# The value projection's last 16 tokens in one stationary tile

## The chip, the cores and the metric

The kernel runs on one core of a Trainium2 chip. The metric is the device time of one execution in microseconds (us); the time before is the median of three runs. The engines are TensorE (PE in the profile, its weight loads PEld), VectorE (DVE), ScalarE (ACT), GpSimd (POOL) and SyncE (SP, which issues DMAs). Each engine works through its own queue of instructions in order; an instruction that waits for another engine holds up what stands behind it.

## What is computed

Two layers of a decoder. In each, a mixer (attention with a forget gate, a convolution module, a short gated convolution) is followed by a feed-forward part. With 16 meta tokens ahead of 512 there are L = 528 tokens of 1024 features.

```python
u = rms_norm(h, pre_g)
z = jnp.einsum("bld,de->ble", u, w_in)
q, k, v, f_logit, a_val, a_gate, sc_b, sc_c, sc_x = jnp.split(z, idx, axis=-1)
log_f = jax.nn.log_sigmoid((f_logit + b_forget).astype(jnp.float32))
y_attn = forgetting_attention(q.reshape(hs), k.reshape(hs), v.reshape(hs), log_f)
```

The change touches the product that makes v (512 columns, 8 heads of 64) and f_logit (8 columns).

## The kernel before

Each float32 operand of a product is kept as two tiles, a rounded one (hi) and the remainder (lo), and a product is made as three: hi x hi, hi x lo and lo x hi, all added up in one PSUM bank. The normalised input u is held as `uhi` and `ulo`, 128 features by 8 k tiles by 528 tokens.

`v_proj(j)` makes v for four heads at a time (j = 0 and 1; for j = 0 with the 8 columns of the forget gate, so 264 columns, else 256). Its stationary operand is u, its moving operand the weights, so the tokens come out on the partitions: 528 tokens are four blocks of 128 (b = 0 to 3) and one of 16 (b = 4). Each block is 8 k tiles x 3 = 24 products (line 1407) into one of the three banks that the ring "mm" hands round; q, k and the other projections use the same ring. When a block is done, `out` (line 1389) copies v on ACT into `vals` (line 1392), and for j = 0 adds the gate's bias on DVE into `fx` (line 1396); both read the block's bank, and the bank is free when both have ended. `forget_gate` starts when all five `fx` are there: some small operations on ACT and DVE, the last of DVE's being the additions into `fpre` (line 1435), and then the products of lines 1439 and 1440 on PE.

The tiles of the mixer are set up on POOL just before, by `mset` (a memset, line 448), in the order of the code: `vals`, `fx`, `p4`, `causal`, then the four `kh` and `qh` pairs, then `dm0` and `dm1`. In both layers the value projection with j = 0 is the first work on PE after them.

What sets the order on the other engines is a planner. A call of `act(...)`, `dve(...)` or `gp(...)` hands it an operation with an estimated duration, what it waits for and a priority (lower goes first); a generator such as `v_proj` yields after each k tile, and the planner's clock `flow` decides which thread's products, and which operation of which engine, are emitted next. An engine's queue then has that order on the chip, whatever the real times are. Calls made outside the planner, such as the memsets of `mset`, cost nothing on its clock. The planner has DVE fill the gaps between urgent operations with the convolution's taps (line 1153, 60 per layer, in two chains) and has ACT and DVE split the coming weights (lines 789 and 793).

`y_pair(i)` hands out a pair of tiles of 128 x 528 from eight tags; the mixer's outputs are kept in them. `y_pair(7)` is written only near the end of the mixer.

Of the kernel before, what the change touches and what calls it, by code (L numbers as in the profile page):

```python
# [10 lines left out]
F32 = mybir.dt.float32  # L11
# [5 lines left out]
P = 128  # L17
D = 1024
KD = D // P
L = 528  # L20
# [3 lines left out]
HEADS = 8  # L24
DH = 64
# [43 lines left out]
_COLS = {}  # L69
# [287 lines left out]
def mm_us(n, k=P):  # L357

    return max(n / 2400 + 0.012, 0.00086 * k)
# [7 lines left out]
def act_us(n):  # L367
    return 0.17 + 0.0009 * n


def dve_us(n):
    return 0.17 + 0.00101 * n


def stt_us(n):
    return 0.22 + 0.00102 * n
# [13 lines left out]
def tile_hybrid_trunk(ctx: ExitStack, tc: tile.TileContext, xT, wflat, pv_d, out):  # L390
    nc = tc.nc
# [3 lines left out]
    def T(pool, shape, dt, tag, bufs=None):  # L395
        uid[0] += 1
        kw = {} if bufs is None else {"bufs": bufs}
        return pool.tile(list(shape), dt, tag=tag, name=f"{tag}_{uid[0]}", **kw)
# [29 lines left out]
    def mmt(i=None):  # L428

        if i is None:  # L430
            i = PAIRS[n_pairs[0] % 2]
            n_pairs[0] += 1
        return psum[:, i:i + 2]
# [4 lines left out]
    for l in range(DEPTH):  # L438
        pv = T(const, [P, NPV], F32, f"pv{l}")
# [7 lines left out]
    def mset(t, val):  # L447
        nc.gpsimd.memset(t.bitcast(F32), val)
# [33 lines left out]
    flow = Flow()  # L482


    uhi = T(keep, [P, KD, L], F32R, "uhi")
    ulo = T(keep, [P, KD, L], F32R, "ulo")
# [4 lines left out]
    def load_h(pool, src, prio=0):  # L491

        t = T(pool, [P, KD, L], F32, "h", 1)
        at = {(hf, k0): flow.op("sp", dma_us(2 * H), lambda k0=k0, hf=hf: nc.sync.dma_start(
            t[:, k0:k0 + 2, half_sl(hf)], src[:, k0:k0 + 2, half_sl(hf)]), prio=prio + 3 * hf, lat=dma_lat(2 * H))
            for hf in range(2) for k0 in range(0, KD, 2)}
        return t, at
# [187 lines left out]
    def next_w():  # L685
        prefetch(1 + AHEAD)
        return ready.popleft()[1]

    def act(us, fn, *after, **kw):
        return flow.op("act", us, fn, after, **kw)  # L690

    def dve(us, fn, *after, **kw):
        return flow.op("dve", us, fn, after, **kw)

    def gp(us, fn, *after, **kw):
        return flow.op("pool", us, fn, after, **kw)
# [127 lines left out]
    def flow_w():  # L824

        b = blocks_w(1)[0]
        yield [b.tok]
        return b
# [17 lines left out]
    def two(t):  # L846
        return t.rearrange("p (a b) -> p a b", a=2)
# [277 lines left out]
    def mixer(l, ypool, first, close_first, spans, front, rzs, u_at):  # L1125
        pv, pg = pvs[l]
# [119 lines left out]
        ap = ms.enter_context(tc.tile_pool(name=f"ap{l}", bufs=1, side="right", reuse_waits="tile"))  # L1246
# [4 lines left out]
        def bank(kind):  # L1251

            slot = yield from flow.grab(banks[kind])
            return psum[:, slot.buf], slot
# [83 lines left out]
        vals = T(ap, [P, 5, HEADS, VW], F32, "vals")  # L1338
        mset(vals[:, 4], 0.0)
        mset(vals[:, :, :, DH:], 1.0)  # L1340
        fx = T(ap, [P, 5, HEADS], F32, "fx")
# [31 lines left out]
        for j in range(2):  # L1373
            dm = T(ap, [P, L], F32R, f"dm{j}")
            mset(dm[:, :N_META], 0.0)
            dms.append(dm)
        g_hl = [T(mp, [P, L], F32, "sq", 2)[:HEADS].bitcast(F32R) for _ in range(2)]

        v_at = {}

        def v_proj(j):
            blks = []
            for _ in range(2):
                blks.append((yield from flow_w()))
            wv = [b.w for b in blks]
            nw = wv[0][0].shape[-1]
            fs, vs = [], []

            def out(b, n, ps, tok):
                src = ps[:n, :256].rearrange("p (h d) -> p h d", d=DH)  # L1390
                c = _COLS["b_forget"]
                a = act(act_us(256), lambda: nc.scalar.copy(vals[:n, b, 4 * j:4 * j + 4, :DH], src), tok)
                r = []
                vs.append(a)
                if nw > 256:
                    r.append(dve(0.2, lambda: nc.vector.tensor_add(fx[:n, b, :], ps[:n, 256:nw], pv[:n, c:c + HEADS]),
                                 tok, prio=0))
                    fs.append(r[-1])
                return [a] + r

            for b in range(5):
                n = min(P, L - P * b)
                ps, slot = yield from bank("mm")
                for k in range(KD):
                    w = wv[k // 4]
                    for p, (wi, ui) in enumerate(((0, 0), (0, 1), (1, 0))):
                        nc.tensor.matmul(ps[:n, :nw],  # L1407
                                         lhsT=(uhi, ulo)[ui][:, k, P * b:P * b + n],
                                         rhs=w[wi][:, k % 4, :],
                                         start=k == 0 and p == 0, stop=k == KD - 1 and p == 2)  # L1410
                    tok = flow.mm(3 * mm_us(nw))
                    if k < KD - 1:
                        yield
                if b == 4:
                    for blk in blks:
                        blk.slot.close(tok)
                slot.close(*out(b, n, ps, tok))
                yield
            v_at[j] = vs
            if nw > 256:  # L1420
                flow.thread(forget_gate(fs), True)
# [391 lines left out]
        def fill():  # L1813

            for kind, j in mixer_steps(l)[2:]:
                if kind == "v":
                    yield from v_proj(j)
                elif kind == "q":
                    yield from q_proj(j)
                elif kind == "k":  # L1820
                    yield from k_proj(j)
                elif kind == "pw":
                    blk = yield from flow_w()
                    flow.thread(conv_tail(blk), True)
                else:
                    if j == 1 and kind == "sc_c":
                        yield [When(lambda: [zero] if 0 in sc_done else None)]
                    yield from proj({"sc_c": sc_c, "sc_x": sc_x, "sc_b": sc_b}[kind](j))
# [17 lines left out]
        for i, f in enumerate(sums_at(l, 1)):  # L1846
            copies, *adds = sum_steps(l, f)
            tok = flow.op("sp", 2.0, copies, (Tok(flow.pe + SUM_AT[i]),), prio=8, lat=SUM_LAT)
            for op in adds:
                tok = gp(SUM_US, op, tok, prio=8, lat=SUM_LAT)  # L1850
# [169 lines left out]
    def y_pair(i):  # L2020
        t = T(ypool, [P, 2, L], F32R, f"y{i}")
        return t[:, 0], t[:, 1]
# [6 lines left out]
    with tc.tile_pool(name="pre", bufs=2, reuse_waits="tile") as sp, tc.manual_schedule(engines=every):  # L2029
# [7 lines left out]
        h, h_at = load_h(sp, xT)  # L2037
# [5 lines left out]
        for k in range(KD):  # L2043
            hk, hi, lo, gc = h[:, k, :H], u_raw[0][k], u_raw[1][k], g0[:, k:k + 1]
            c = act(act_us(H) + 0.06, lambda hk=hk, hi=hi, gc=gc: nc.scalar.activation(hi, hk, AF.Copy, scale=gc),
                    h_at[0, k - k % 2], prio=0)
            d = dve(stt_us(H), lambda hk=hk, hi=hi, lo=lo, gc=gc: nc.vector.scalar_tensor_tensor(
                lo, in0=hk, scalar=gc, in1=hi.bitcast(F32), op0=ALU.mult, op1=ALU.subtract), c, prio=0)
# [45 lines left out]
    for l in range(DEPTH):  # L2094
        pv, pg = pvs[l]
# [14 lines left out]
        with ms, tc.manual_schedule(engines=every):  # L2110
            flow.yields = YM
            y, y_at, early = mixer(l, ypool, first, close_pools, i_spans, front, rzs, u_at)
# [5 lines left out]
        with tc.tile_pool(name=f"fp{l}", bufs=2, reuse_waits="tile") as fp:  # L2118
# [35 lines left out]
            with tc.manual_schedule(engines=every):  # L2154
                flow.yields = YF
                h, h_at = load_h(fp, xT if l == 0 else h_dram)
# [188 lines left out]
            for part, nf in enumerate(PARTS):  # L2345
                for f in range(f0, f0 + nf):
# [15 lines left out]
                    for i in (2 * f, 2 * f + 1):  # L2362
# [5 lines left out]
                        w = next_w()  # L2368
                        ps = mmt((6, 2)[i % 2]) if ts else mmt()
# [17 lines left out]
                if part < len(PARTS) - 1:  # L2387
# [3 lines left out]
                    for some in ((0, 1), *((m,) for m in range(2, KD))):  # L2391
# [12 lines left out]
                        for m, ps in zip(some, tiles):  # L2404
                            if final:
                                d, src = yp[:, m, t0:], ps[:, 0, :2 * fw]
                            else:
                                d, src = two(yp[:, m, t0:]), ps[:, :, :fw]
# [82 lines left out]
```

## Time and profile before

| | us |
|---|---|
| three runs | 1262.51, 1263.30, 1263.05 |
| median | 1263.05 |
| span of the profiled execution | 1262.4 |
| granted TensorE clock, mean | 0.999 |
| value projection j = 0, first layer, on PE | 49.10 to 63.5 |
| value projection j = 0, second layer, on PE | 676.96 to 691.5 |
| value projection j = 1, first layer, among attention | 123.3 to 149 |

The profile is that of one execution; it gives its span, from the first to the last instruction, and no other time of it. All times in rows are us from the start of the span. A timeline row has the start, the time busy, the engine and line, the operation, what it writes and reads (out<-in), sizes and count, and in brackets the idle time of the engine just before and what ended it. "x3" is three instructions in one row. A row of the waits has the engine and line that waited and what it waited for, the total, the count and the longest. A row of groups ends with the busy time and mean ns of one, and the idle time before. A PE product's time overlaps with its neighbours', so that the distance of two starts, and not the length, is what one costs.

### The profile page before, as it was taken

The page shows a single profiled execution, that of the slowest core. Times are in us where ns is not written, and L with a number is a line of the kernel's source. Part 1 is how long each engine was busy: PE and PEld are TensorE (multiplying, and loading weights), DVE is VectorE, ACT ScalarE, POOL GpSimd, SP SyncE. Part 2 cuts the span into 40 slices and gives each one's busy share as a digit, 9 for nine tenths or more (in the row PEclk, how much of TensorE's full clock was granted, in tenths as well). Part 3 has the DMA queues.
Part 4 walks back from the last instruction along what each step waited for, and adds up shares of the span by engine and source line. Part 5 has one row for each costly group of instructions (what it writes and reads, how often), then busy time and mean ns, then how long its engine had stood idle before and what let it go on. Part 6 is the DMA issues. An engine that isn't in the chain of part 4 may idle for free.

```text
span 1262.4 us, 24292 instructions
## 1 busy us (share of the span) xinstructions
PE 1243.7 (99%) x9554; PEld 1194.0 (95%) x9554; DVE 926.1 (73%) x1581; ACT 710.3 (56%) x1377; POOL 174.6 (14%) x360
## 2 busy tenths in 40 slices
PE   8999999999999999999999999999999999999997
PEld 8998898999999999999999988999999899989997
DVE  7887866589874776487688878656799748756964
ACT  7254576655444663476673545775554447526763
POOL 1323411001111001010003244120021000000000
PEclk9999999999999999999999999999999999999999
DMA  7357551726648755776652584547166565465611
GB/s 245 82 155 173 126 119 44 259 87 149 186 147 334 244 193 149 240 195 169 208 189 67 156 194 110 144 111 241 71 163 176 146 218 170 153 223 182 203 60 67
DMA packets 80755, 206.59 MB, mean 164 GB/s; under 512 B 8624, under 2 KB 18992, under 8 KB 80128
## 3 DMA queue, kind: packets, MB, share of 16 engines
q1 hardware_dynamic: 66976, 168.20, 42.1%
q0 software_dynamic: 13664, 36.84, 13.0%
q8 instruction: 75, 1.23, 0.4%
q14 instruction: 40, 0.33, 0.1%
HBM read 170.82 MB, written 50.60 MB: 175 GB/s over the span
## 4 chain that ended last, share of the span: by engine, by line
PE 89%; DVE 3%; issue 3%; DMA 2%; ACT 2%; POOL 1%; SPq 0%; DVEq 0%; POOLq 0%; ACTq 0%
PE psum L837 58%; PE psum L2288 17%; PE psum L1407 5%; PE psum L1671 3%; PE psum L1637 2%; PE psum L974 1%; PE psum L1593 1%; DMA raw<-in_w_dram 1%; PE psum L1737 1%; PE psum L1323 1%; DMA w_split<-slo 0%; DMA h<-in_w_dram 0%; POOL dm L1608 0%; DVE yp L1050 0%; DMA h<-in_x_dram 0%
## 5 line engine op out<-in xcount | busy, mean ns | idle before, releaser
L837 PE MATMUL psum<-y,whi 128*128 128x264 f32 (+3 forms) x1968 | 383.8, 299 | 0.8 <-DVE zs L989 0.7
L837 PEld LDWEIGHTS psum<-y,whi 128*128 128x128 f32 x1968 | 305.6, 188 | 13.8 <-DVE zs L989 0.9
L837 PE MATMUL psum<-uhi,whi 128*128 128x264 f32 (+1 forms) x1168 | 292.1, 289 | 1.5 <-ACT uhi L2069 0.7
L837 PE MATMUL psum<-ulo,whi 128*128 128x264 f32 (+1 forms) x1168 | 285.7, 284 | 0.6 <-DVE ulo L2071 0.4
L837 PE MATMUL psum<-uhi,wlo 128*128 128x264 f32 (+1 forms) x1168 | 285.1, 283 | 0.0
L837 PE MATMUL psum<-y,wlo 128*128 128x264 f32 (+3 forms) x984 | 273.7, 297 | 0.3 <-DVE wlo L793 0.3
L837 PEld LDWEIGHTS psum<-uhi,whi 128*128 128x128 f32 x1168 | 201.5, 188 | 6.2 <-issue 1.6
L837 PEld LDWEIGHTS psum<-ulo,whi 128*128 128x128 f32 x1168 | 201.6, 188 | 1.3 <-DVE ulo L2071 0.6
L837 PEld LDWEIGHTS psum<-uhi,wlo 128*128 128x128 f32 x1168 | 201.3, 188 | 0.0
L837 PEld LDWEIGHTS psum<-y,wlo 128*128 128x128 f32 x984 | 177.8, 188 | 5.8 <-DVE wlo L793 0.6
L2173 DVE SCALAR_TENSOR_TENSOR c<-zs,pv,c 128x528 f32<-128x528 f32 (+1 forms) x176 | 130.6, 756 | 23.5 <-ACT c L2171 22.2
L652 ACT CAST whi<-raw 128x1024 fp32r<-128x1024 f32 (+1 forms) x65 | 66.1, 1020 | 97.1 <-PE psum L837 74.5
L793 DVE TENSOR_TENSOR wlo<-raw,whi 128x1024 fp32r<-128x1024 f32 (+2 forms) x80 | 95.6, 1203 | 29.7 <-ACT whi L789 29.2
L789 ACT CAST whi<-raw 128x1024 fp32r<-128x1024 f32 (+2 forms) x80 | 81.7, 1031 | 24.9 <-PE psum L837 18.0
L653 DVE TENSOR_TENSOR wlo<-raw,whi 128x1024 fp32r<-128x1024 f32 (+1 forms) x65 | 76.9, 1183 | 21.1 <-ACT whi L652 21.0
L1153 DVE SCALAR_TENSOR_TENSOR cacc<-apad,pv,cacc 128x528 f32<-128x528 f32 x120 | 87.6, 772 | 0.1
L2288 PE MATMUL psum<-uhi,whi 128*128 128x258 f32 (+1 forms) x252 | 71.3, 284 | 0.0
L2288 PE MATMUL psum<-ulo,whi 128*128 128x258 f32 (+1 forms) x252 | 71.2, 283 | 0.0
L2288 PE MATMUL psum<-uhi,wlo 128*128 128x258 f32 (+1 forms) x252 | 70.7, 283 | 0.0
L2171 ACT ACTIVATE c<-zs,pv 128x528 f32<-128x528 f32 (+1 forms) x88 | 63.0, 727 | 6.8 <-DVE zs L2136 2.7
L2206 POOL COPY cols<-y 128x1 f32<-128x1 f32 x24 | 17.2, 716 | 335.8 <-ACT y L2187 335.5
L2288 PE MATMUL psum<-t,shi 128*128 128x258 f32 (+1 forms) x336 | 63.2, 283 | 0.0
(273 smaller groups left out, 2323.9 us busy)
## 6 DMA issues: line engine op xcount, KB each, us to landing
raw<-in_w_dram SPq DMA_DIRECT2D x114, 512.0 KB, 4.5
raw<-in_w_dram SPq DMA_DIRECT2D x30, 448.0 KB, 5.1
h<-in_w_dram SPq DMA_DIRECT2D x25, 512.0 KB, 4.5
raw<-w_sum SPq DMA_DIRECT2D x21, 512.0 KB, 5.4
h<-w_sum SPq DMA_DIRECT2D x21, 512.0 KB, 4.8
h<-in_w_dram POOLq DMA_DIRECT2D x16, 512.0 KB, 4.6
w_sum<-h POOLq DMA_DIRECT2D x16, 512.0 KB, 6.4
w_sum<-in_w_dram SPq DMA_DIRECT2D x26, 256.0 KB, 5.2
```

The costliest lines, as they stand in the source:

```text
L652: nc.scalar.copy(hi[:, :sz], raw[:, :sz])
L653: last_low[0] = nc.vector.tensor_sub(lo[:, :sz], raw[:, :sz], hi[:, :sz].bitcast(F32))
L789: nc.scalar.copy(box["hi"][:, :sz], box["raw"][:, :sz])
L793: nc.vector.tensor_sub(lo[:, :sz], box["raw"][:, :sz], box["hi"][:, :sz].bitcast(F32))
L837: nc.tensor.matmul(d, lhsT=w[a][:, k, cols], rhs=rhs(b, k, hf), start=start and i == 0 and p == 0, stop=stop and i == n - 1 and p == 2)
L1153: nc.vector.scalar_tensor_tensor(conv[j], in0=src, in1=conv[j], scalar=col("a_dw_w", CK * j + i), op0=ALU.mult, op1=ALU.add)
L1407: nc.tensor.matmul(ps[:n, :nw], lhsT=(uhi, ulo)[ui][:, k, P * b:P * b + n], rhs=w[wi][:, k % 4, :], start=k == 0 and p == 0, stop=k == KD ...
L1637: nc.tensor.matmul(s, lhsT=k[:, ka:ka + kn], rhs=q[:, s0:qz], start=i == 0, stop=i == 1)
L1671: nc.tensor.matmul(acc[:, s0 - qa:qz - qa], lhsT=vals[:, b].rearrange("p h d -> p (h d)")[:, o:o + P], rhs=box["p"], start=b == 0, stop=b ...
L2171: nc.scalar.activation(dst, src[:, 2:2 + 2 * fw], AF.Copy, scale=wtap(2, t))
L2173: nc.vector.scalar_tensor_tensor(dst, in0=src[:, i:i + 2 * fw], scalar=wtap(i, t), in1=dst, op0=ALU.mult, op1=ALU.add)
L2288: nc.tensor.matmul(psum[:, bank, :n7], lhsT=w[a][:, k0 + k, :], rhs=rhs(b, k), start=start and k == 0 and p == 0, stop=stop and k == K2 - ...
```

## The change

For the block of 16 tokens, the high and the low part of u are put side by side in one stationary tile: 48 columns, high in 0 to 15, zeros in 16 to 31, low in 32 to 47. One product with the high weights then makes both hi x hi and lo x hi, on partitions 0 to 15 and 32 to 47 of the bank; a second with the low weights makes hi x lo (and lo x lo beside it). So 16 products take the place of 24, and the rows from partition 32 on are added to the first ones at the end (`out_tail`): an ACT copy into `low`, then one DVE add for v and two small ones for the gate. The tile is borrowed from `y_pair(7)`: a memset on POOL and two ACT copies, asked for once in a layer, ahead of the value projection.

```diff
@@ -1374,6 +1374,11 @@
             dm = T(ap, [P, L], F32R, f"dm{j}")
             mset(dm[:, :N_META], 0.0)
             dms.append(dm)
+        spare_y = y_pair(KD - 1)[0]
+        tail_u = spare_y[:, :KD * 48].rearrange("p (k n) -> p k n", n=48)
+        mset(tail_u, 0.0)
+        tail_at = [act(0.3, lambda i=i, t=t: nc.scalar.copy(tail_u[:, :, 32 * i:32 * i + L - 4 * P], t[:, :, 4 * P:]), prio=2)
+                   for i, t in enumerate((uhi, ulo))]
         g_hl = [T(mp, [P, L], F32, "sq", 2)[:HEADS].bitcast(F32R) for _ in range(2)]
 
         v_at = {}
@@ -1386,7 +1391,25 @@
             nw = wv[0][0].shape[-1]
             fs, vs = [], []
 
+            def out_tail(b, n, ps, tok):
+                to = vals[:n, b, 4 * j:4 * j + 4, :DH]
+                src = ps[:n, :256].rearrange("p (h d) -> p h d", d=DH)
+                c = _COLS["b_forget"]
+                low = T(ap, [32, 256 + HEADS], F32, "low", 1)[:n, :nw]
+                heads = low[:, :256].rearrange("p (h d) -> p h d", d=DH)
+                a = act(act_us(nw), lambda: nc.scalar.copy(low, ps[32:32 + n, :nw]), tok)
+                vs.append(dve(dve_us(256), lambda: nc.vector.tensor_add(to, src, heads), a))
+                r = []
+                if nw > 256:
+                    r.append(dve(0.2, lambda: nc.vector.tensor_add(fx[:n, b, :], ps[:n, 256:nw], pv[:n, c:c + HEADS]),
+                                 tok, prio=0))
+                    fs.append(dve(0.2, lambda: nc.vector.tensor_add(fx[:n, b, :], fx[:n, b, :], low[:, 256:nw]),
+                                  *r, a, prio=0))
+                return [a, vs[-1]] + r
+
             def out(b, n, ps, tok):
+                if b == 4:
+                    return out_tail(b, n, ps, tok)
                 src = ps[:n, :256].rearrange("p (h d) -> p h d", d=DH)
                 c = _COLS["b_forget"]
                 a = act(act_us(256), lambda: nc.scalar.copy(vals[:n, b, 4 * j:4 * j + 4, :DH], src), tok)
@@ -1403,12 +1426,18 @@
                 ps, slot = yield from bank("mm")
                 for k in range(KD):
                     w = wv[k // 4]
-                    for p, (wi, ui) in enumerate(((0, 0), (0, 1), (1, 0))):
+                    if b == 4:
+                        if k == 0:
+                            yield tail_at
+                        for p in range(2):
+                            nc.tensor.matmul(ps[:48, :nw], lhsT=tail_u[:, k, :], rhs=w[p][:, k % 4, :],
+                                             start=k == 0 and p == 0, stop=k == KD - 1 and p == 1)
+                    for p, (wi, ui) in enumerate(((0, 0), (0, 1), (1, 0)) if b < 4 else ()):
                         nc.tensor.matmul(ps[:n, :nw],
                                          lhsT=(uhi, ulo)[ui][:, k, P * b:P * b + n],
                                          rhs=w[wi][:, k % 4, :],
                                          start=k == 0 and p == 0, stop=k == KD - 1 and p == 2)
-                    tok = flow.mm(3 * mm_us(nw))
+                    tok = flow.mm((3 if b < 4 else 2) * mm_us(nw))
                     if k < KD - 1:
                         yield
                 if b == 4:
```

Three places show what the engines' queues hold now, all in the first layer's mixer (the second has the same). In the rows a tile's numbers tell its instances apart, and lines behind the change carry the changed kernel's numbers (1415 is 1392 of before, 1419 is 1396, 1464 is 1435, 1541 is 1512, 1546 is 1517).

ACT's queue around the first evacuations, before and then now; `sccx` is a short-convolution tile that comes just ahead, `y_100` is the borrowed tile, `whi` a weight split, `fe` the forget gate:

```order
L1195 COPY sccx_669<-psum_67 128x264
L1392 COPY vals_681<-psum_67 128x4x64 x4
L1392 COPY vals_681<-psum_67 16x4x64
L1427 ACTIVATE fe_884<-fx_684 128x40
L789 CAST whi_900<-raw_406 128x1024
L1428 ACTIVATE fe_884<-fe_884 128x40
L789 CAST whi_914<-raw_588 128x1024
```

```order
L1195 COPY sccx_669<-psum_67 128x264
L1380 COPY y_100_732<-uhi_108 128x8x16
L1380 COPY y_100_732<-ulo_109 128x8x16
L1415 COPY vals_681<-psum_67 128x4x64 x4
L1400 COPY low_879<-psum_67 16x264
L789 CAST whi_891<-raw_406 128x1024
L1456 ACTIVATE fe_880<-fx_684 128x40
L789 CAST whi_909<-raw_588 128x1024
```

The two copies into the borrowed tile stand ahead of the evacuations of all four wide blocks; the first of the two waits for POOL.

POOL's queue at the end of the mixer's memsets, now; `q_96` is the last of the `qh` tiles, `w_sum` a transfer for a later stage:

```order
L448 MEMSET q_96_710 32x528 x2
L448 MEMSET dm_98_728 128x16
L448 MEMSET dm_99_730 128x16
L448 MEMSET y_100_732 128x384
L534 DMA w_sum_11_104_737<-in_w_dram 128x2x512
```

The memset of the borrowed tile has come in as the last one, behind all that were there.

DVE's queue from the third block's `fx` to the forget gate's last additions, before and then now; `cacc` are the convolution's taps, `wlo` weight splits, `q_91` and `q_93` the low parts of q:

```order
L1396 TENSOR_TENSOR fx_684<-psum_67,pv_3_69 128x8
L1153 SCALAR_TENSOR_TENSOR cacc_135<-apad_133,pv_3_69,cacc_135 128x528
...
L1433 MEMSET fpre_885 128x8
L1396 TENSOR_TENSOR fx_684<-psum_67,pv_3_69 16x8
...
L793 TENSOR_TENSOR wlo_931<-raw_588,whi_914 128x1024
L1432 TENSOR_TENSOR fe_884<-fe_884,fx_684 128x40
L1517 SCALAR_TENSOR_TENSOR q_91_705<-psum_67,q_90_704 64x264
L1517 SCALAR_TENSOR_TENSOR q_93_707<-psum_67,q_92_706 64x264
L1435 TENSOR_TENSOR fpre_885<-fpre_885,fe_884 128x8 x4
```

```order
L1404 TENSOR_TENSOR fx_684<-psum_67,pv_3_69 16x8
L1406 TENSOR_TENSOR fx_684<-fx_684,low_879 16x8
L1401 TENSOR_TENSOR vals_681<-psum_67,low_879 16x4x64
...
L793 TENSOR_TENSOR wlo_928<-raw_588,whi_909 128x1024
L1546 SCALAR_TENSOR_TENSOR q_91_705<-psum_67,q_90_704 64x264
L1546 SCALAR_TENSOR_TENSOR q_93_707<-psum_67,q_92_706 64x264
L1461 TENSOR_TENSOR fe_880<-fe_880,fx_684 128x40
L1464 TENSOR_TENSOR fpre_881<-fpre_881,fe_880 128x8 x3
L1546 SCALAR_TENSOR_TENSOR q_91_705<-psum_67,q_90_704 64x264
L1464 TENSOR_TENSOR fpre_881<-fpre_881,fe_880 128x8
```

Two operations have come in behind the small block's `fx`, of the twelve taps from the first `fx` to `fpre` ten are left in this stretch, and a third piece of q has moved ahead of the last addition. On PE the gate's two products (lines 1439 and 1440) now stand behind fifteen products of k, where they stood behind nine.

## The prediction

> **What bounds the kernel now.** I read the page first: engine totals, then the chain of work that ended last.
>
> ```profile
> span 1262.4 us, 24292 instructions
> PE 1243.7 (99%) x9554; PEld 1194.0 (95%) x9554; DVE 926.1 (73%) x1581; ACT 710.3 (56%) x1377; POOL 174.6 (14%) x360
> PE 89%; DVE 3%; issue 3%; DMA 2%; ACT 2%; POOL 1%; SPq 0%; DVEq 0%; POOLq 0%; ACTq 0%
> ```
>
> TensorE (PE) carries 89% of the chain, so a product taken out of its stream should shorten the kernel by its pitch, and a wait put into it should lengthen it. The busy share alone proves little, because product times overlap; the starts show the pitch. Next come PE's waits in the stretch with the value projections, for the first layer (45 to 215 us) and the second (672 to 845).
>
> ```profile
> PE psum L1593 <- issue: 1.2, 1, 1.2
> PE psum L1617 <- POOL dm L1608: 0.4, 1, 0.4
> PE psum L1323 <- ACT q L1619: 0.4, 1, 0.4
> PE psum L1671 <- POOL pf L1651: 0.3, 1, 0.3
> ...
> PE psum L1593 <- DMA k<-pair_hi: 1.1, 1, 1.1
> PE psum L1617 <- POOL dm L1608: 1.0, 1, 1.0
> PE psum L1323 <- ACT q L1619: 0.4, 1, 0.4
> PE psum L1671 <- POOL pf L1651: 0.3, 1, 0.3
> ```
>
> 2.3 and 2.8 us of waiting in 170 us each: PE sets the time there, and little idle time is left to absorb a new wait.
>
> **What is removed.** The timeline of PE shows the first layer's blocks of the first value projection.
>
> ```profile
> 57.70 0.29 PE L1407 MATMUL psum<-whi,uhi 128*128 128x264 f32 x1
> ...
> 60.50 0.28 PE L1407 MATMUL psum<-wlo,uhi 128*128 128x264 f32 x1
> 60.62 0.28 PE L1407 MATMUL psum<-whi,uhi 128*16 128x264 f32 x1
> ...
> 63.41 0.29 PE L1407 MATMUL psum<-wlo,uhi 128*16 128x264 f32 x1
> ...
> 685.56 0.29 PE L1407 MATMUL psum<-whi,uhi 128*128 128x264 f32 x1
> ```
>
> Block 3 (128 tokens wide) has 24 products between 57.70 and 60.50: (60.50 - 57.70) / 23 = 0.122 us. Block 4 (16 wide) has 24 from 60.62 to 63.41: 2.79 / 23 = 0.121. The pitch is the same at 16 and at 128 columns of the stationary tile, so 48 columns cost 0.121 too. Eight products go at each of four places (two projections, two layers): 32 x 0.121 = **-3.9 us**.
>
> [...] The trace has 121 ns, and that is used.
>
> **What is added: a wait at the head of ScalarE's queue.** The two copies into the new tile stand on ACT ahead of the copies that evacuate blocks 0 to 3, and they wait for a memset that POOL does last of all its mixer memsets. These are POOL's rows around that place, in both layers, and the groups of memsets in the second layer.
>
> ```profile
> 57.36 0.16 POOL L448 MEMSET dm<- 128x16 f32 x2
> 57.92 1.24 POOL L534 DMA_DIRECT2D w_sum<-in_w_dram  x1 [0.39 <-issue]
> ...
> 688.06 0.17 POOL L448 MEMSET dm<- 128x16 f32 x2
> ...
> L448 POOL MEMSET q<- 32x528 f32 x8 | 4.3, 532 | 0.3
> L448 POOL MEMSET dm<- 128x16 f32 x2 | 0.2, 118 | 0.1
> ```
>
> The new memset follows dm, from 57.53 (57.36 + 0.16, rounded) and 688.23. Between 118 ns at 16 columns and 532 at 528, 384 columns lie at 118 + 368 / 512 x 414 = 416 ns: it ends at 57.94 and 688.64. Bounds 0.12 and 0.53.
>
> ```profile
> 52.06 0.37 ACT L1392 COPY vals<-psum 128x256 f32<-128x256 f32 x1 [2.90 <-PE psum L1407]
> 54.98 0.38 ACT L1392 COPY vals<-psum 128x256 f32<-128x256 f32 x1 [2.55 <-PE psum L1407]
> ...
> 679.92 0.37 ACT L1392 COPY vals<-psum 128x256 f32<-128x256 f32 x1 [7.20 <-PE psum L1407]
> ...
> 123.20 0.27 ACT L1684 ACTIVATE sq<-psum 128x128 f32<-128x128 f32 x1
> 123.36 0.25 ACT L1685 COPY yta<-psum 64x128 f32<-64x128 f32 x1
> ```
>
> So the evacuation of block 0, which began at 52.06 and 679.92, has to wait behind copies that cannot begin before 57.94 and 688.64. Two copies of 128 elements take 0.16 + 0.25 = 0.4 us by the last two rows (bounds 0.3 and 0.75, two of the 0.37 us copies), the evacuation 0.37. Then VectorE (DVE):
>
> ```profile
> 52.53 0.17 DVE L1396 TENSOR_TENSOR fx<-psum,pv 128x8 f32<-128x8 f32 x1 [0.90 <-ACT vals L1392]
> 52.62 1.56 DVE L1210 SCALAR_TENSOR_TENSOR sccx<-cxp,pv,sccx 128x528 f32<-128x528 f32 x2
> 54.10 0.76 DVE L1153 SCALAR_TENSOR_TENSOR cacc<-apad,pv,cacc 128x528 f32<-128x528 f32 x1
> 55.39 0.17 DVE L1396 TENSOR_TENSOR fx<-psum,pv 128x8 f32<-128x8 f32 x1 [0.53 <-ACT vals L1392]
> 55.47 2.12 DVE L1153 SCALAR_TENSOR_TENSOR cacc<-apad,pv,cacc 128x528 f32<-128x528 f32 x3
> 58.31 0.17 DVE L1396 TENSOR_TENSOR fx<-psum,pv 128x8 f32<-128x8 f32 x1 [0.72 <-ACT vals L1392]
> ...
> 61.22 0.17 DVE L1396 TENSOR_TENSOR fx<-psum,pv 128x8 f32<-128x8 f32 x1 [0.71 <-ACT vals L1392]
> ...
> 64.17 0.15 DVE L1396 TENSOR_TENSOR fx<-psum,pv 16x8 f32<-16x8 f32 x1 [0.73 <-ACT vals L1392]
> ```
>
> The forget-gate add (fx) of a block always starts after ACT's copy of the same bank, and it blocks DVE's queue while it waits. Three banks serve the projection, so block 3 needs block 0's bank, which fx frees. With 0.15 us for three hand-overs (0.03 to 0.1 each between the ACT and DVE rows), block 3 starts at 57.94 + 0.40 + 0.37 + 0.17 + 0.15 = 59.03 in place of 57.70: **+1.3 us**. In the second layer POOL starts its memsets later against PE: 688.64 + 1.09 = 689.73 in place of 685.56: **+4.2 us**. The bounds of memset and copies move each by -0.4 to +0.5. Blocks 1 and 2 are long computed and cover nothing; block 4 needs fx of block 1, 2.3 us of DVE work behind the first fx, and block 3's 2.9 us hide that.
>
> **The backlog behind fx.** DVE comes out of that wait with its first fx at 58.76, 6.2 us late. Queued behind it are the convolution taps, the weight splits and the additions (fpre) that the forget gate's products need:
>
> ```profile
> 69.09 0.77 DVE L1435 TENSOR_TENSOR fpre<-fpre,fe 128x8 f32<-128x8 f32 x4
> ...
> 70.47 0.31 PE L1439 MATMUL psum<-fe,tri 128*128 128x40 f32 x2
> 70.60 0.39 PE L1440 MATMUL psum<-fpre,ones_r 128*128 128x40 f32 x2
> ```
>
> Before, fpre ended at 69.86 and PE wanted it at 70.60. From 52.53 to 69.86 are 17.3 us, 2.7 of them waits (0.53 + 0.72 + 0.71 + 0.73), which vanish since the blocks are then ready: 14.6 us of work. Of this, two taps move behind (2 x 0.7 = -1.4), and about 1.0 comes in: a small add (0.15), the add of the low half (at most the 0.42 of an add of 264 columns), and one piece of q that is now ahead (0.43). fpre ends at 58.76 + 14.2 = 73.0. PE arrives at 70.60 + 1.33 (bank) - 0.97 (eight products) + 0.73 (six products that now stand ahead of the gate) = 71.7. It waits **1.3 us**. Both engines run from the first fx on, so the second layer's wait is the same: +2.6 together. Bounds: nothing, if DVE's order leaves it faster than summed; 2.0 each, if the last of the four waits (0.73) stays. The weight splits come out just in time by the same sum, so that a later DVE would be felt there first and not twice. After the gate, DVE and PE are late alike.
>
> The second value projection adds an ACT copy in place of one and one DVE add, late in the layer, with no queue standing: no cost beside its saving. The borrowed tile is written again long after its last reader. The planner also reorders products behind that projection (head 7 begins some twenty rows earlier in the first layer); of the waits above only 0.7 us a layer lie there to be gained, and the largest present wait, 1.2 us, bounds what a layer may lose. I take zero.
>
> **Sum**: -3.9 + 1.3 + 4.2 + 2.6 = +4.2 us on the profiled 1262.4, which lies 0.65 below the median 1263.05; carried over to the median, **1267.3**. Nearly all is paid in the second layer.
>
> **Rivals.**
> - *The backlog does not reach the gate.* If fpre is there when PE comes, only the bank waits stay: 5.5 - 3.9 = +1.6, 1264.7. Speaks for it: two taps are moved out of the way. Against: the sum leaves it 1.3 us late.
> - *Faster: memsets run quicker while DVE stands still.* POOL's memsets overlap DVE's taps before; in the change DVE waits from 52.5. If DVE slowed them to double, the nine of them left in the first layer and some thirteen in the second would end 2.4 and 3.5 us sooner (0.27 each): bank waits 0 and 0.7, gate waits about 0.3 in all, sum -2.9, 1260.2. It decides from about 0.2 us a memset on. Against it stands a row from the start, where DVE is idle: 0.23 at 128 columns, no less than the 0.21 that lies between the rows above.
>
> ```profile
> 2.18 0.23 POOL L448 MEMSET ones_r<- 128x128 f32 x1
> ```
>
> [...]
> - *Slower still: the reordered tails or a backlog on the weight splits cost another wait of 1.2 us a layer:* 1269.7.
> - That 48 columns run slower than 16 is excluded by the equal pitch at 128.
>
> **How the numbers follow.** A measurement can tell about 0.2% (2.5 us) from no change: faster is below 1260.5, slower above 1265.6. Forecast 0.58 (own range 1265.6 to 1269), backlog absorbed 0.18, faster 0.09, slower still 0.15. Slower: 0.58 + 0.15, less 0.03 for a forecast that lands lower: 0.70; same 0.18 + 0.03 = 0.21; faster 0.09. Low end: 5.5 - 0.8 (bounds) + 0 - 3.9 - 1.4 (reordering) = -0.6, 1262.5. High end: 5.5 + 1.0 + 4.0 - 3.9 = +6.6, 1269.7, and half a microsecond for the tails: 1270.2.
>
> **What would show it.** In the trace after: the two copies at 58.0 and 688.7 on ACT with a wait on POOL; block 0's evacuation at 58.4 and 689.1; a gap of 1.3 and 4.2 us on PE before block 3; a wait of 1.3 us on DVE at the gate's products; 16 products at 0.121 us for block 4. The prediction is wrong if the copies start much before 57.9, if block 3 starts on time, or if the delay at 700 us is not there at the end.

## The result, and the profile after

| | us |
|---|---|
| before, median of 4 runs beside the change | 1262.94 |
| after, median of 4 runs | 1274.58 (1274.30 to 1275.09) |
| ratio | 1.0093, 95% interval 1.0078 to 1.0107 |
| span of the profiled execution, before and after | 1262.4 and 1273.4 |

The change is 11.6 us slower; 4.2 were forecast. The page of the kernel after has these totals and this chain:

```profile
span 1273.4 us, 24240 instructions
PE 1244.6 (98%) x9522; PEld 1195.3 (94%) x9522; DVE 928.0 (73%) x1587; ACT 711.3 (56%) x1381; POOL 173.6 (14%) x362
PE 89%; DVE 4%; ACT 2%; POOL 2%; DMA 2%; issue 1%; SPq 0%; DVEq 0%; POOLq 0%; ACTq 0%
```

32 products fewer, and the span is 11.0 us longer; DVE and POOL hold a point more of the chain each. PE's waits after, first layer (45 to 215 us) and then second (672 to 860), with what was waited for, the total, the count and the longest:

```profile
PE psum L1700 <- ACT yta L1714: 1.2, 2, 1.0
PE psum L1436 <- DVE fx L1419: 1.1, 1, 1.1
PE psum L837 <- DVE pair_lo L1574: 1.1, 1, 1.1
PE psum L1469 <- DVE fpre L1464: 0.8, 1, 0.8
...
PE psum L1436 <- DVE fx L1419: 4.0, 1, 4.0
PE psum L1818 <- DVE pair_lo L1574: 1.0, 1, 1.0
PE psum L837 <- DVE y L1311: 0.9, 2, 0.6
```

The rows on `fx` (block 3's bank) and `fpre` (the gate) were foreseen. Those on `yta`, `pair_lo` and `y` are new and lie behind the second value projection. The foreseen wait can be followed link by link in the timelines of POOL, ACT and DVE. The first five rows are of the first layer; the last two, of the second, are the last pair of the older full-width memsets and the first `fx` behind them:

```profile
58.52 0.42 POOL L448 MEMSET y<- 128x384 f32 x1
58.98 0.30 ACT L1380 CAST y<-uhi 128x128 fp32r<-128x128 f32 x1 [8.71 <-POOL y L448]
59.18 0.29 ACT L1380 CAST y<-ulo 128x128 fp32r<-128x128 f32 x1
59.38 0.91 ACT L1415 COPY vals<-psum 128x256 f32<-128x256 f32 x3
59.85 0.17 DVE L1419 TENSOR_TENSOR fx<-psum,pv 128x8 f32<-128x8 f32 x1 [7.12 <-ACT vals L1415]
...
691.13 1.09 POOL L448 MEMSET q<- 32x528 f32 x2
...
693.69 0.17 DVE L1419 TENSOR_TENSOR fx<-psum,pv 128x8 f32<-128x8 f32 x1 [10.57 <-POOL y L448]
```

The chain of both layers then has block 3 (24 products) and the small block (16):

```profile
60.07 3.19 PE psum L1436 x24
63.26 1.94 PE psum L1433 x16
...
693.91 5.47 PE psum L1436 x24
699.38 1.93 PE psum L1433 x16
```

Block 3's 24 products take 3.19 us in the first layer and 5.47 in the second, though the instructions are the same. The windows of the second layer show why. A row has the window and its duration, the busy time of PE, PEld, DVE, ACT and POOL, and then the clock granted to PE.

```profile
686.00:692.20 6.20, 3.88 (x32) 3.67 (x31) 0.00 (x0) 0.00 (x0) 5.78 (x11) 1.00 0.00 1
692.20:695.60 3.40, 1.69 (x7) 1.69 (x8) 1.87 (x4) 1.32 (x5) 1.73 (x5) 0.50 0.24 19
695.60:699.00 3.40, 3.40 (x18) 3.40 (x17) 3.40 (x8) 0.00 (x0) 0.00 (x0) 0.50 0.84 135
699.00:702.00 3.00, 3.00 (x27) 2.99 (x26) 2.90 (x8) 1.03 (x3) 0.86 (x1) 0.99 0.28 35
```

PE fell idle at 689.9 and was busy for only 3.88 us of the first window. The clock was at half from 692.2 to 699.0, and nearly all of block 3's products lay in that stretch: 0.220 us from start to start, in place of 0.121.

To see where the time goes, take a product's start after less the start of the same product before, counted from the first one and leaving out the eight missing ones of each small block. The growth of that lag, by stretches of the time before:

| stretch, us | what lies there | foreseen | measured |
|---|---|---|---|
| 0 to 40 | opening, ahead of any change | 0 | +1.1 |
| 57 to 59 | bank wait, layer 1 | +1.3 | +1.4 |
| 59 to 66 | small block, j = 0 | -1.0 | -1.0 |
| 66 to 75 | gate | +1.3 | +1.35 |
| 75 to 146 | a present wait gets shorter | 0 | -0.5 |
| 146 to 216 | small block, j = 1, and what follows | -1.0 | **+2.6** |
| 420 to 445 | a present wait gets shorter | 0 | -0.9 |
| 680 to 692 | bank wait, block 3, small block, layer 2 | +3.2 | **+5.6** |
| 692 to 715 | gate | +1.3 | +0.05 |
| 715 to 748 | a present wait gets shorter | 0 | -0.8 |
| 748 to 866 | small block, j = 1, and what follows | -1.0 | **+1.7** |
| 866 to the end | | 0 | +0.3 |
| sum | | +4.2 | +11.0 |

### The profile page after: what moved, and what is told of

It is laid out like the page before. It is cut to its first block, busy times and chain, and to the rows that moved or that the text cites. A ratio compares the mean times of both kernels' runs of the same rounds, so it can differ in the third digit from the quotient of the medians.

```text
span 1273.4 us, 24240 instructions
## 1 busy us (share of the span) xinstructions
PE 1244.6 (98%) x9522; PEld 1195.3 (94%) x9522; DVE 928.0 (73%) x1587; ACT 711.3 (56%) x1381; POOL 173.6 (14%) x362
## 4 chain that ended last, share of the span: by engine, by line
PE 89%; DVE 4%; ACT 2%; POOL 2%; DMA 2%; issue 1%; SPq 0%; DVEq 0%; POOLq 0%; ACTq 0%
PE psum L837 60%; PE psum L2317 17%; PE psum L1700 3%; PE psum L1436 2%; PE psum L1666 2%; PE psum L974 1%; PE psum L1622 1%; POOL q L448 1%; POOL k L448 1%; PE psum L1433 1%; PE psum L1766 1%; DMA raw<-in_w_dram 0%; PE psum L1323 0%; DMA h<-in_x_dram 0%; DMA q<-pair_hi 0%
```

## The experiments

Two theories of the loss behind the second projection came first. **O** (order): the queues' new order costs there by itself. **B** (backlog): ACT and DVE carry the lateness of the memset into it. Four kernels separate them. The first asks for the borrowed tile and its memset ahead of `vals`, and keeps the change's order; the second keeps the late memset and tells the planner the old durations and operations, which gives the old order; the third does both (`lows` copies the low half and, for j = 1, adds it to v behind that; `adds` makes the three additions of j = 0 as one operation); the fourth is the work of before in the change's order. The traces bear the orders out: PE, DVE and ACT run the rows of the change in `new_order` and those of before in `old_plan_first`, apart from the small block's own and a few others.

```diff
 memset_first
+        spare_y = y_pair(KD - 1)[0]
+        tail_u = spare_y[:, :KD * 48].rearrange("p (k n) -> p k n", n=48)
+        mset(tail_u, 0.0)
         vals = T(ap, [P, 5, HEADS, VW], F32, "vals")
 old_plan (the three lines stay where they were), old_plan_first
-        tail_at = [act(0.3, lambda i=i, t=t: nc.scalar.copy(...), prio=2)
+        for i, t in enumerate((uhi, ulo)):
+            nc.scalar.copy(tail_u[:, :, 32 * i:32 * i + L - 4 * P], t[:, :, 4 * P:])
...
-                a = act(act_us(nw), lambda: nc.scalar.copy(low, ps[32:32 + n, :nw]), tok)
+                a = act(act_us(256), lows, tok)
+                fs.append(dve(0.2, adds, tok, prio=0))
-                    tok = flow.mm((3 if b < 4 else 2) * mm_us(nw))
+                    tok = flow.mm(3 * mm_us(nw))
 new_order
+        tail_at = [act(0.3, lambda: None, prio=2) for _ in range(2)]
...
+                vs.append(dve(dve_us(256), lambda: None, a))
+                    for p, (wi, ui) in enumerate(((0, 0), (0, 1), (1, 0))):
```

> The memset of the borrowed tile is asked for ahead of POOL's other mixer memsets; everything else is the change, in its order. So ACT's two copies should not wait, and block 3 of the first value projection should start on time in both layers. Theory O (the products that the planner reordered behind the second value projection cost 3.6 us in the first layer and 2.65 in the second by themselves): bank waits, slow products and gate wait go (1.4 + 6.6 + 1.3), the 1.3 us that later waits had absorbed of them come back: 1274.6 - 9.3 + 1.3 = 1266.6, with both losses behind the second projection still there. Theory B (those losses are the backlog of ACT and DVE from the wait, carried on): they go too, about 1261.

> The change's 16 products, copies and adds, with the memset late as in the change, but the planner is told what it was told before (24 products' time, one ACT and one DVE operation for the small block), so that every queue has the order of before. Theory O: the losses behind the second value projection (3.6 and 2.65 us) go, the waits before it stay: 1274.6 - 6.2 + 0.9 (a wait at 437 us that had absorbed part comes back) = 1269.3. Theory B: the losses stay, 1274 to 1275.

> The change's work in the order of before, and the memset first: neither the wait nor the reordering. Both theories: the saving of 32 products alone, 1262.9 - 3.9 = 1259.0. If instead the added copies and adds of the small block cost time on ACT and DVE themselves, 1262 or more.

> The work of before (24 products for the small block, no borrowed tile, no copies into it) with the planner told what the change tells it, so that the queues have the change's order. Theory O: slower than before by the losses behind the second projection, 3.6 + 2.65 less the 0.9 that the wait at 437 us absorbs: about 1268. Theory B: as before, 1262 to 1264.

| kernel | us | ratio to before, interval |
|---|---|---|
| memset_first | 1265.75 | 1.0028 (1.0017 to 1.0039) |
| old_plan | 1280.14 | 1.0142 (1.0122 to 1.0161) |
| old_plan_first | 1269.97 | 1.0054 (1.0042 to 1.0067) |
| new_order | 1270.25 | 1.0053 (1.0039 to 1.0066) |

The memset's place was worth 8.8 us (1274.58 - 1265.75). `new_order` speaks for O: it has no borrowed tile, no copies into one and 24 products, and is slower than before all the same. Its PE waits are those of the change (line 1690 is 1700 there, 1564 is 1574), first layer and then second:

```profile
PE psum L1690 <- ACT yta L1704: 1.2, 2, 1.0
PE psum L837 <- DVE pair_lo L1564: 1.0, 1, 1.0
...
PE psum L1808 <- DVE pair_lo L1564: 1.0, 1, 1.0
PE psum L837 <- DVE y L1311: 0.9, 2, 0.6
```

DVE's timeline shows how one arises, before and then in `new_order`:

```profile
168.17 0.43 DVE L1295 SCALAR_TENSOR_TENSOR rs_t<-rs_t,rs_r 128x264 f32<-128x264 f32 x1
168.57 0.43 DVE L1545 SCALAR_TENSOR_TENSOR pair_lo<-psum,pair_hi 128x264 fp32r<-128x264 f32 x1
168.92 0.89 DVE L1773 SCALAR_TENSOR_TENSOR cacc<-cacc,pg,rs_t 128x264 f32<-128x264 f32 x2
```

```profile
168.20 0.43 DVE L1295 SCALAR_TENSOR_TENSOR rs_t<-rs_t,rs_r 128x264 f32<-128x264 f32 x1
168.67 0.90 DVE L1792 SCALAR_TENSOR_TENSOR cacc<-cacc,pg,rs_t 128x264 f32<-128x264 f32 x2
169.73 0.43 DVE L1564 SCALAR_TENSOR_TENSOR pair_lo<-psum,pair_hi 128x264 fp32r<-128x264 f32 x1 [0.16 <-ACT pair_hi L1561]
```

`pair_lo`, which frees a bank, now stands behind two 0.45 us additions and an ACT operation that comes later too, and ends 1.16 us later; PE stops. The lag's growth over the two stretches, with the 0.97 saved there added back, is what the rest of each kernel costs there (1.7 us of `memset_first`'s 5.3 are a halved clock, told in the last section):

| kernel | 146 to 216 | 748 to 866 |
|---|---|---|
| after | 3.6 | 2.7 |
| new_order (nothing saved) | 3.6 | 2.7 |
| memset_first | 5.3 | 2.7 |
| old_plan_first | 5.0 | 5.1 |

After and `new_order` agree in both: **6.3 us are the order's**. The medians fit roughly: 1262.93 less the 3.9 saved and with the 6.3 makes 1265.3, and `memset_first` took 1265.75, though its trace too has present waits that get shorter. `new_order`'s median is 7.3 above that of before; its traced execution took 1268.38, and what the others take beyond that is in no trace. The old order with the change's work (`old_plan`, `old_plan_first`) loses even more, which neither theory had: `old_plan_first` was expected at 1259.0, `old_plan` at 1269.3 or at 1274 to 1275. The waits of `old_plan_first` have one row of 3.2 us in each layer:

```profile
PE psum L1705 <- POOL pf L1685: 3.2, 1, 3.2
```

POOL's rows (first `before`, then `old_plan_first`) show a selection, the causal mask of an exponential block, and DVE's rows of `old_plan_first` what runs meanwhile:

```profile
151.45 0.56 POOL L1651 TENSOR_SCALAR_AFFINE_SELECT pf<-pf 128x128 f32<-128x128 f32 x1 [6.13 <-ACT pf L1644]
```

```profile
149.49 4.44 POOL L1685 TENSOR_SCALAR_AFFINE_SELECT pf<-pf 128x128 f32<-128x128 f32 x2 [5.32 <-ACT pf L1678]
...
148.14 0.41 DVE L1403 TENSOR_TENSOR vals<-psum,low 16x256 f32<-16x256 f32 x1
148.48 0.75 DVE L1153 SCALAR_TENSOR_TENSOR cacc<-apad,pv,cacc 128x528 f32<-128x528 f32 x1
149.15 1.21 DVE L793 TENSOR_TENSOR wlo<-raw,whi 128x1024 fp32r<-128x1024 f32 x1
150.29 0.75 DVE L1153 SCALAR_TENSOR_TENSOR cacc<-apad,pv,cacc 128x528 f32<-128x528 f32 x1
150.97 1.21 DVE L793 TENSOR_TENSOR wlo<-raw,whi 128x1024 fp32r<-128x1024 f32 x1
152.10 1.43 DVE L1153 SCALAR_TENSOR_TENSOR cacc<-apad,pv,cacc 128x528 f32<-128x528 f32 x2
```

The row of two selections holds one of 4.19 us and one of 0.29. The long one ended at 153.69, DVE's row at 153.53; the second layer's took 4.19 too. Then the clock is halved on top, by the windows:

```profile
150.30:153.70 3.40, 0.20 (x2) 0.00 (x0) 3.23 (x5) 0.40 (x1) 3.40 (x2) 1.00 0.59 173
153.70:157.10 3.40, 3.36 (x11) 2.70 (x12) 0.00 (x0) 0.29 (x1) 0.52 (x2) 0.50 0.39 140
```

`old_plan` has the late memset, this stall in both layers and three stretches of half clock, and is the slowest.

The clock and the selection were tested next, each by itself. One kernel gives PE something to do in the second layer's bank wait; two take the two things that `old_plan_first` has at that place, the DVE addition and the missing products, into the kernel before, one at a time; and one makes the change in the first projection only.

```diff
 fill_wait (on the change)
+                if l == 1 and j == 0 and b == 3:
+                    for _ in range(32):
+                        nc.tensor.matmul(psum[:, 7, :nw], lhsT=uhi[:, 0, :P], rhs=wv[0][0][:, 0, :], start=True, stop=True)
 add_second (on before, in the evacuation, behind ACT's copy)
...
+                    if b == 4 and j == 1:
+                        spare = T(ap, [32, 256], F32, "low", 1)[:n]
+                        nc.vector.tensor_add(spare.rearrange("p (h d) -> p h d", d=DH), src, vals[:n, b, 4 * j:4 * j + 4, :DH])
 short_second (on before)
+                        if b == 4 and j == 1 and p == 1:
+                            continue
 first_half (on old_plan_first)
-                if b == 4:
+                if b == 4 and j == 0:
                     return out_tail(b, n, ps, tok)
... (and the same condition where the products are made)
```

> The change, with 32 products into an unused PSUM bank put ahead of block 3 of the first value projection in layer 2, so that TensorE works through the 4.2 us in which it waits for that bank. Clock theory (TensorE stood idle for 4.2 us, so it was then granted half its clock for 6.8 us): the granted clock stays 1.0 there, the 24 products of block 3 take 0.121 us each in place of 0.220, about -2.4 us; the gate's wait of 1.3 us, which the slow products had covered, comes back; together about 1.2 us less than the change, 1273.4 (1272.4 to 1273.9). Rival (block 3 is slow for another cause, its weights or its bank): pitch stays 0.220 and the time stays 1274.6.

> The kernel before, with one DVE addition more (16x256, read from the bank and from what ACT has just copied, into an unused tile) right behind the evacuation of the small block of the second value projection, in both layers; 24 products as before. In the kernel with the change's work in the old order the POOL selection right behind that place took 4.19 us in place of 0.56. Theory A (the addition alone closes the 0.57 us gap in DVE's row through which POOL got in): about +5 us in each layer, 1272.9. Theory S (it needs the 0.97 us that the small block saves, so that DVE runs later against ACT; 0.34 of addition leaves 0.2 us of gap): no selection over 1.3 us and the time within 0.5 us of the kernel before, 1262.9 to 1263.5.

> The kernel before, leaving out in the second value projection, for the last 16 tokens only, the product of the high part of the weights with the low part of the tokens: 16 products in place of 24 there, nothing added, the order of all queues as before, in both layers. Theory S (0.97 us saved on TensorE and ACT closes the 0.57 us gap in DVE's row): the selection takes 4.2 us in each layer, TensorE waits 3.2 us for it and is then granted half its clock, about +4 us a layer in place of -0.97, 1270 to 1271. Theory A (it is the added DVE work): 1262.9 less what of 2 x 0.97 isn't absorbed later, 1261.0 to 1262.5.

> The change in the first of the two value projections alone, the memset moved ahead of the others and the queues in the order of the kernel before: 16 products saved in each layer, ACT's copies and DVE's additions of that projection are there. If the losses behind the second projection come from the new order and from the selection there, neither is left: the time is 1262.9 - 2 x 0.97, less what the waits at 108, 437 and 746 us absorb, 1261.0 to 1262.3. If ACT's copies and the memset cost by themselves, or the 0.97 saved earlier closes DVE's gap too: 1264 or more.

| kernel | us | ratio to before, interval |
|---|---|---|
| fill_wait | 1273.77 | 1.0085 (1.0070 to 1.0101) |
| add_second | 1263.03 | 1.0001 (0.9992 to 1.0010) |
| short_second | 1261.78 | 0.9990 (0.9981 to 0.9999) |
| first_half | 1260.89 | 0.9982 (0.9974 to 0.9991) |

`fill_wait`, the windows around the same place, then the chain and the gate's row of the waits:

```profile
692.20:695.60 3.40, 3.24 (x27) 3.03 (x26) 1.88 (x4) 1.32 (x5) 1.71 (x5) 1.00 0.17 10
695.60:699.00 3.40, 3.40 (x31) 3.39 (x30) 3.40 (x8) 0.38 (x1) 0.00 (x0) 1.00 0.91 143
```

```profile
693.90 3.18 PE psum L1439 x24
```

```profile
PE psum L1472 <- DVE fpre L1467: 0.8, 1, 0.8
```

The clock stays at 1.00, block 3 starts at the same 693.9 and takes 3.18 us, 2.3 less. PE then waits for the gate, which it does not in the change's second layer. In the lag, 680 to 692 adds 3.4 in place of 5.6, and 692 to 715 adds 1.4 in place of 0.05. The idle time, not the block, caused the slow products. The median is 0.8 below the change's and within what was expected, but the two intervals overlap: here the trace decides, not the time.

Neither the addition nor the missing products alone lengthen the selection by more than 0.3 us: POOL's rows of `add_second` and then of `short_second`, the same place:

```profile
150.22 0.62 POOL L1657 TENSOR_SCALAR_AFFINE_SELECT pf<-pf 128x128 f32<-128x128 f32 x1 [6.13 <-ACT pf L1650]
```

```profile
149.94 0.84 POOL L1653 TENSOR_SCALAR_AFFINE_SELECT pf<-pf 128x128 f32<-128x128 f32 x1 [5.18 <-ACT pf L1646]
```

So A fell, and S, which had asked for the missing products only, fell as well. `first_half`, with neither at that place, took 1260.89 (expected 1261.0 to 1262.3) and is 1.9 us faster than before.

Last, whether the moment of issue or the addition in DVE's row decides. Two kernels put one and three tiny ACT copies ahead of the exponential; the third takes the addition out of DVE's row and puts it behind.

```diff
 nudge, nudge3 (on old_plan_first)
+                if (hd, qa, b) == (4, P, 1):
+                    nc.scalar.copy(T(ap, [32, 256 + HEADS], F32, "low", 1)[:16, :16], ident[:16, :16])
 late_add (on old_plan_first)
-                        nc.vector.tensor_add(to, src, heads)
+                        nc.scalar.copy(to, src)
+                        late.append(lambda: nc.vector.tensor_add(to, to, heads))
...
+            while late and b == 4 and hd >= 4:
+                late.pop()()
```

> The change's work in the order of before with the memset first (the kernel that took 1269.97), and one tiny ACT copy more (16x16, into an unused tile) right ahead of the exponential whose selection took 4.19 us, in both layers; nothing else. There the selection was issued 0.34 us after a 1.21 us DVE instruction began and got in only when DVE's row of five instructions ended; in the other kernels selections issued 0.38 us or later got in at the end of the DVE instruction that was running. Theory M (it is a matter of the moment of issue): the selection is issued some 0.15 us later, takes under 1.3 us, and the time is that of the kernel before less about 2 us a layer, less what later waits absorb: 1258.5 to 1261. Theory D (DVE's row, made longer by the saved products and the addition, keeps POOL out whatever the moment): the selection still ends with DVE's row, 4.0 us, 1269 to 1271.

> As the one before, with three such copies in place of one: the selection is issued some 0.4 us later. Theory M: as with one copy, 1258.5 to 1261.3. Theory D: 1269 to 1271, the selection 3.8 us.

> The change's work in both projections, in the order of before with the memset first; of the small block of the second projection ACT copies both halves out of the bank, and DVE's addition is put off behind the row of five instructions that kept POOL out, ahead of the next pair_lo, where DVE stood idle for 1.05 us before. If it takes the addition as well as the saved products to keep POOL out (each alone did not), the selection takes under 1.3 us, and the time is that of the change in the first projection alone, 1260.9, less another 0.97 a layer, with up to 0.36 of ACT's copy given back in each and part absorbed by the later waits: 1259 to 1260.9. Rival (the products saved in both projections keep POOL out without the addition): a selection of over 2 us in each layer, 1264 to 1270.

| kernel | us | ratio to before, interval | long selection, layers 1 and 2 |
|---|---|---|---|
| nudge | 1269.69 | 1.0052 (1.0036 to 1.0067) | 4.11, 4.10 |
| nudge3 | 1265.92 | 1.0022 (1.0013 to 1.0031) | 2.27, 2.27 |
| late_add | 1260.81 | 0.9979 (0.9969 to 0.9988) | none (at most 1.08 there) |

Theory M fell: issued 0.43 us after the weight split began, the selection still lasted to the end of DVE's row (4.11 us). D held for `nudge`; in `nudge3` the selection, issued 0.90 us after the split began, ended behind three of the row's instructions (2.27 us), and the time lies between what M and D gave. POOL and DVE in `late_add`:

```profile
149.10 0.56 POOL L1687 TENSOR_SCALAR_AFFINE_SELECT pf<-pf 128x128 f32<-128x128 f32 x1 [5.55 <-ACT pf L1680]
150.42 1.80 POOL L1687 TENSOR_SCALAR_AFFINE_SELECT pf<-pf 128x128 f32<-128x128 f32 x2 [0.76 <-ACT pf L1680]
...
151.28 1.50 DVE L1153 SCALAR_TENSOR_TENSOR cacc<-apad,pv,cacc 128x528 f32<-128x528 f32 x2
152.70 0.41 DVE L1405 TENSOR_TENSOR vals<-vals,low 16x256 f32<-16x256 f32 x1
```

All 32 products are saved here, and the order of before is kept otherwise: 2.6 us faster than before (1263.41 beside it) of the 3.9 that the products are worth. It is the fastest median of the study, though its interval overlaps that of `first_half`.

## Why the prediction was wrong

**Right.** The saving: each small block took 16 products, 1.94 us in place of some 2.9, -0.97 in the lag. The queue-head wait: foreseen +1.3 and +4.2, measured +1.4 and 4.2 (the product ahead of block 3 started at 689.59, block 3 at 693.91: 4.32 less a pitch of 0.12). Its links came out one by one; the memset took 0.42 against 0.416 worked out. The two copies took 0.50 against 0.40. The gate in the first layer: +1.3, measured 1.35, though not as one wait: PE stood 0.84 us for `fpre` and 0.38 for `gt`, the gate's next step on DVE. That memsets would run quicker while DVE stands was a rival and fell: a pair of POOL's memsets took 1.09 us while DVE stood idle for 10.57 us, 0.53 for each as before.

**Wrong, first: "The planner also reorders products behind that projection ... I take zero."** This term was 3.6 + 2.7 = +6.3 us. The step had bounded a layer's loss by the largest wait present, 1.2 us, and the rival that named these tails took the same figure. That is no bound: in each layer several new waits of 0.3 to 1.1 us arose (on `pair_lo`, `cxp`, `yta` and `rs_t` in the first; on `pair_lo` and `y` in the second), and their sum was more than any one. The rows above show for `pair_lo` how it was put behind others; for the others that is argued, not shown.

**Wrong, second: the bank wait of the second layer was priced by its length alone.** 4.2 us of idle time brought 2.4 us more, since the clock was halved for 6.8 us. The rows of before have no such idle stretch, but the forecast made one.

**Wrong, third and in compensation: the gate's wait in the second layer**, foreseen 1.3, measured 0.05. DVE's work did not slow with TensorE here (three taps took 2.12 us in this stretch as in the first layer); with block 3 slow, `fpre` was there in time. `fill_wait` brings the wait back. The waits that shrank further on took 2.2 off, and the opening and the end put 1.4 on.

That the second projection's added copy and addition cost nothing held in the change's order alone. In the old order they came with a selection of 4.19 us in each layer, and nothing in the prediction told the two cases apart.

So the sum misses 6.3 for the order and 2.4 for the clock, and has 1.3 too much at the gate: 4.2 + 6.3 + 2.4 - 1.3 = 11.6, less 2.2 and with 1.4 it is 10.8, against a measured lag of 11.0.

## What to carry to other kernels

A wait at the head of a queue can cost more than its length: behind 3.2 and 4.2 us in which TensorE stood idle, the clock was halved for 3.4 and 6.8 us here, so count the products there at half clock. Where a planner orders queues, a change in the durations or operations that it is told is a change of its own; keep the old order and place the new work by hand first, and judge the two apart. An operation that is off the path by its engine's share can still come to stand in another engine's way: here 0.4 us more on DVE, with the saved products, came with a POOL selection of 4.19 us in each layer, and moved behind the row it cost nothing of the kind. Look at what runs beside it before giving DVE even 0.4 us.

## What was not expected of the hardware

**The clock was halved behind idle time, for 3.4 or 6.83 us.** In `memset_first` two waits in the first layer were enough:

```profile
198.50:201.90 3.40, 2.04 (x12) 1.31 (x11) 1.18 (x3) 2.95 (x9) 0.29 (x1) 1.00 0.00 0
201.90:205.30 3.40, 3.40 (x9) 2.07 (x9) 1.70 (x4) 1.72 (x5) 0.58 (x2) 0.50 0.00 0
```

PE was busy for 2.04 of 3.40 us, and the next 3.4 us had half the clock: that is the 1.7 us by which `memset_first` exceeds the order's 3.6 in the table. The change has the same two waits at the same place without a halved clock. The stretches of half clock last 3.4 us in `memset_first` and `old_plan_first` and 6.83 us in the change. In the change's trace the clock changed at 692.21, 699.04 and 1272.47: the 573.44 us from the second to the third are 84.0 times the 6.83 from the first to the second, so that steps of half that, 3.413 us, fit all three. Counted in such steps from where the clock changed, both waits of `memset_first` lie in one step. Those of the change lie in two, 200.69 to 204.10 and 204.10 to 207.52, with PE busy for 2.33 and 3.14 us. That the clock goes by such steps, and that the change kept its clock for this reason, is the author's estimate from these times. Busy time is not the whole measure: in the change the step from 1265.65 to 1269.06 had 1.99 us and was followed by full clock. What else counts stays open.

The runs of `memset_first` lay between 1264.61 and 1270.61. The traced one took 1270.61. It has a wait of 1.9 us that ended at 428.9, and the 94 products behind it took 13.45 us, 0.143 us each in place of some 0.12; that the clock was halved there too is an estimate from this and from its mean clock of 0.997, where the other eight have 0.999 to 1.000. No run here moves the steps alone.

**A POOL selection lasted through a whole row of DVE instructions.** In `before`, 27 of the 64 selections of 128x128 in the attention took 0.34 to 1.30 us, the other 37 at most 0.30, and each of the 27 ended 0.15 or 0.16 us after a DVE instruction. At this one place in `old_plan_first` the selection took 4.19 us, and ended 0.16 us after the last of five DVE instructions in a row. That DVE held it back is the author's reading of these end times. Only kernels with both the missing products and the addition ahead of the row did this; why the selection did not end behind one of the four before the last stays open. An unbroken row is not enough: in `add_second`, `short_second` and `late_add` the same five follow one another without a gap, and the selection ended behind the first, after 0.62, 0.84 and 0.56 us. Nor is the moment of issue alone: issued 0.34 and 0.43 us after the split began the selection lasted to the row's end (4.19 and 4.11 us), from 0.52 to 0.82 it ended behind the first, and at 0.90 (`nudge3`) it missed two ends (2.27 us).
